# The norm before the MLP in a two-layer encoder kernel: transposes of the residual's second half grouped in four PSUM banks between halves of up tiles, and the first weight sums moved behind the third up tile

## The chip, the cores and the metric

One core of one Trainium2 chip. The metric is device time in microseconds (us) of one execution; the median of 3 runs of the kernel before is 1730.86 us (1730.69 to 1731.39). The engines are PE (TensorE: matrix products and transposes), DVE (VectorE), ACT (ScalarE), POOL (GpSimd), and SP, whose queue issues most weight loads.

## The reference, cut to what matters

Two layers, 512 positions of 1024 channels, float32. Of each layer only its end matters here:

```python
merged = (gates[:, :, 0] * (y_a @ w_br[l, 0]) + gates[:, :, 1] * (y_b @ w_br[l, 1])
          + gates[:, :, 2] * (y_c @ w_br[l, 2]))
x = x + merged @ w_out[l]
hn = rms_norm(x, ln2[l])
x = x + jnp.square(jax.nn.relu(hn @ w_up[l])) @ w_down[l]
```

`w_up` is 1024x4096 and `w_down` 4096x1024. `rms_norm` divides each row by its root mean square and multiplies by a weight per channel.

## The kernel before, in words

**Products.** Every float32 operand is split in a high and a low part (`split`, `wsplit`): ACT rounds the value to the matmul's format (the high part, `xh`, `wh`), DVE subtracts that from the value (the low part, `xl`, `wl`). A product is then three matmuls, high by high, low by high and high by low (`mm3`, lines 212 to 214). A weight chunk of 128x1024 is loaded by SP (`wr`, line 187; 2 buffers), cast by ACT (line 207) and subtracted by DVE (line 208) into a pair `wh`, `wl` (3 buffers each).

**The residual and its norm.** `proj_tok` makes `merged @ w_out` by halves of 512 channels (`fl` 0 and 1), in four PSUM banks, one for each 128 positions. DVE adds each bank to the residual `xr` (line 1108), ACT takes sums of squares (line 314). The MLP needs the residual with channels on the partitions, so `turn` (line 316) transposes it on PE: a half gives 4 tiles `xT` of 128x512, each from 4 transposes of 128x128 (line 327) into one PSUM bank. Of each tile ACT makes `xh` (line 265) and DVE `xl` (line 266), both reading the bank, which is free for another tile after that. The first half goes through the two banks with the tag `c`, the second through the two banks with the tag `s`. PSUM has 8 banks here: two each of tags `m`, `a`, `c`, `s`.

**The MLP.** The 4096 hidden channels go in four quarters (`qd`), each of 8 up tiles (`f` 0 to 7) and then a down product. An up tile is a PSUM bank of 128 hidden channels by 512 positions, the sum over `k` of 8 channel tiles, 24 matmuls of 128x512, in a bank of tag `m`: tiles `k` 0 to 3 come from the residual's first half and 4 to 7 from its second. ACT takes Relu and Square (lines 1171, 1172), and `left_first` / `left_second` make splits and sums of the squares for the down product, which is a seven-product scheme (Strassen's) over 2x2 blocks. That scheme also needs sums of the blocks of the down weights. Those are 8 chunks `wq`, loaded by `uload` on SP's queue (line 197); their pool opens when `Y2`, which holds the operand of `w_out`, is closed. `early_sums` (lines 403 and 405) makes 4 sums of 128x1024 of them on DVE, in place or into two further buffers.

**What sets the order.** Each engine runs its instructions in a fixed order, which a scheduler decides as the program is built, from its own estimate of a timeline and from priorities (`hp()` raises one). `tc.issue_after(x)`, which the change uses, is a context whose instructions are ordered behind instruction `x` on their engine. In the order before, up tiles 0 and 1 of the first quarter are interleaved with each other and with the transposes of the second half, and the 4 early sums stand on DVE among the 4 `xl` of that half. The source calls `early_sums` after up tile 4.

Of the kernel before, what the change touches and what calls it, by code (L numbers as in the profile page):

```python
# [6 lines left out]
F32 = mybir.dt.float32  # L7
# [3 lines left out]
ALU = mybir.AluOpType  # L11

P = 128
S = 512
D = 1024
KT = D // P
# [13 lines left out]
def ap_of(t, off, dims):  # L30
    return bass.AP(tensor=t.tensor, offset=t.offset + off, ap=[t.ap[0]] + dims)
# [29 lines left out]
def trunk(tc, xT, xt, ws, vec, fnb, bsb, snk, wst, rope, cmask, amask, ident, out):  # L61
    nc = tc.nc
# [52 lines left out]
    def Z():  # L115
        z4[1] += 1
        return z4[0][:, (z4[1] - 1) % 4]
# [4 lines left out]
    def SM(tag, w):  # L122
        return pad.tile([P, w], F32, tag="sm_" + tag, bufs=4 if tag == "lb" else NSM, name=nm(tag))
# [4 lines left out]
    def PT(tag, name):  # L128
        return ps.tile([P, S], F32, tag="p_" + tag, bufs=BANKS[tag], name=nm(name))
# [3 lines left out]
    def hp():  # L133

        return tc.high_priority() if boost[0] else contextlib.nullcontext()
# [36 lines left out]
    def ln_ap(which, l, kt):  # L172
        c = {"ln1": 0, "ln2": 16, "fn": 32}[which] + (l * 8 if which != "fn" else 0) + kt
        return vec_t[:, c:c + 1]
# [7 lines left out]
    def wload(*key):  # L182
        if key in ready:
            return ready.pop(key)
        with hp():
            raw = sb.tile([P, CW], F32, tag="wr", bufs=WR, name=nm("wr"))
            nc.sync.dma_start(raw, ws[CHUNK[key]])
            return wsplit(raw)
# [12 lines left out]
    def whl():  # L201
        return (sb.tile([P, CW], F32R, tag="wh", bufs=WB, name=nm("wh")),
                sb.tile([P, CW], F32R, tag="wl", bufs=WB, name=nm("wl")))

    def wsplit(raw):
        hi, lo = whl()
        nc.scalar.copy(hi, raw)  # L207
        nc.vector.tensor_tensor(lo, raw, hi.bitcast(F32), ALU.subtract)  # L208
        return hi, lo

    def mm3(pt, whi, wlo, xhi, xlo, first, last):
        nc.tensor.matmul(pt, whi, xhi, start=first, stop=False)  # L212
        nc.tensor.matmul(pt, whi, xlo, start=False, stop=False)  # L213
        nc.tensor.matmul(pt, wlo, xhi, start=False, stop=last)  # L214

    def proj(xs, name, *key, bank="m"):

        return proj_w(xs, name, wload(*key), bank=bank)

    def proj_w(xs, name, w, koff=0, bank="m"):  # L220
        hi, lo = w
        pt = PT(bank, name)
        for k, x in enumerate(xs):
            c = slice((koff + k) * P, (koff + k + 1) * P)
            mm3(pt, hi[:, c], lo[:, c], x[0], x[1], k == 0, k == len(xs) - 1)
        return pt
# [32 lines left out]
    def split(src, hi, lo, scale=None):  # L259

        if scale is None:
            nc.scalar.copy(hi, src)  # L262
            nc.vector.tensor_tensor(lo, src, hi.bitcast(F32), ALU.subtract)
        else:
            nc.scalar.activation(hi, src, AF.Copy, scale=scale)
            nc.vector.scalar_tensor_tensor(lo, src, scale, hi.bitcast(F32), ALU.mult, ALU.subtract)  # L266


    def rstd_c(pt, n):
# [36 lines left out]
    def norm_tok(which, l, xr, keep):  # L306

        n = Norm()
        n.xs, n.xf = [None] * KT, [None] * KT
        n.ss = SM("ss8", 8)  # L310

        def add(t, fl):
            j = T("jk", "jk")
            nc.scalar.activation(j, xr[t][fl], AF.Square, accum_out=n.ss[:, t * 2 + fl:t * 2 + fl + 1])

        def turn(fl, ts, bank="s"):

            w = len(ts) * P
            c0 = ts[0] * P
            for d in range(4 * fl, 4 * fl + 4):  # L320
                if n.xs[d] is None:
                    n.xs[d] = (T("x", "xh", F32R), T("x", "xl", F32R))
                    if keep:
                        n.xf[d] = Z() if d < 4 else T("l", "xf")
                pt = PT(bank, "xT")
                for i, t in enumerate(ts):
                    nc.tensor.transpose(pt[:, i * P:(i + 1) * P], xr[t][fl][:, (d % 4) * P:(d % 4 + 1) * P], id_t)
                src = pt[:, 0:w]
                parts = [x[:, c0:c0 + w] for x in n.xs[d]]
                if keep:  # L330
                    xf = n.xf[d][:, c0:c0 + w]
                    nc.scalar.activation(xf, src, AF.Copy, scale=ln_ap(which, l, d))
                    split(xf, *parts)
                else:
                    split(src, *parts, ln_ap(which, l, d))

        def end():
            s = SM("s4", 4)
            nc.vector.tensor_tensor(s, ap_of(n.ss, 0, [[2, 4]]), ap_of(n.ss, 1, [[2, 4]]), ALU.add)
            n.rc = rstd_c(s, D)  # L340

        n.add, n.turn, n.end = add, turn, end
        return n

# [8 lines left out]
    HT = 2 * P  # L353
# [4 lines left out]
    def left_first(new, u):  # L358

        p1 = new().rearrange("p (a b) -> p a b", a=2)  # L360
        split(u[:, 0:HT], p1[:, 0], p1[:, 1])
        sb_ = part["wq"].tile([P, 2, HT], F32, tag="sf", bufs=2, name=nm("sf"))
        nc.vector.tensor_tensor(sb_[:, 0], u[:, 0:HT], u[:, HT:], ALU.subtract)
        return {1: (p1[:, 0], p1[:, 1]), "u": u, "s": sb_}

    def left_second(new, h, v):
        V = nc.vector
# [32 lines left out]
    def early_sums(raw):  # L400
        b11, b12, b22, b21, t1 = raw
        for i in range(2):
            nc.vector.tensor_tensor(t1[i], b11[i], b12[i], ALU.add)
        for i in range(2):
            nc.vector.tensor_tensor(b12[i], b12[i], b22[i], ALU.add)
# [267 lines left out]
    raw, hi, lo = sb.tile([P, CW], F32, tag="wr", bufs=WR, name=nm("wr")), *whl()  # L673
    for i in range(2):
        c = slice(i * S, (i + 1) * S)
# [26 lines left out]
    for l in range(DEPTH):  # L702
        xs = n1.xs
# [53 lines left out]
        if l == 0:  # L757
            raw = uload(l, "un", 0)
# [62 lines left out]
        for u in range(3):  # L821
# [7 lines left out]
            raw = nxt  # L829
# [40 lines left out]
        for g in range(4):  # L870
            pt = PT("s", "mx")
# [64 lines left out]
        pt = PT("c", "vT")  # L936
# [162 lines left out]
        xr = [[T("l", "xr"), T("l", "xr")] for _ in range(4)]  # L1099
# [3 lines left out]
        n2 = norm_tok("ln2", l, xr, False)  # L1103
        for fl in range(2):
            pts = proj_tok(ms, "wo", (l, "wo", fl), fl, None if fl else lambda: turn_sum(1))
            for t in range(4):
                with hp():
                    nc.vector.scalar_tensor_tensor(xr[t][fl], pts[t], 0.5, xr[t][fl], ALU.mult, ALU.add)
                    n2.add(t, fl)
            with hp():  # L1110
                n2.turn(fl, range(4), "s" if fl else "c")
        with hp():
            n2.end()
        r2 = SM("r2", 4)
        nc.vector.tensor_tensor(r2, n2.rc, n2.rc, ALU.mult)
        nr2 = SM("r2", 4)
# [7 lines left out]
        last = l + 1 == DEPTH  # L1124
# [33 lines left out]
        for qd in range(4):  # L1158
            hs, nh = [], [0]

            def new():
                nh[0] += 1
                return T("jk" if nh[0] == 1 else "rb" if nh[0] > 27 else "l2" if nh[0] > 23 else "h", "sh", F32R)

            for f in range(8):
                pt = proj(n2.xs, f'up{qd}', l, "up", qd, f)
                if f == 0:
                    raw = uload(l, "dn", qd)
                u = Z()
                with hp():  # L1170
                    nc.scalar.activation(u, pt, AF.Relu)  # L1171
                    nc.scalar.activation(u, u, AF.Square)
                    if f % 2 == 0:
                        hs.append(left_first(new, u))
                    else:
                        left_second(new, hs[-1], u)
                if f == 4:
                    early_sums(raw)
            if qd == 3:
                if last:  # L1180
                    for fl in range(2):
                        fn_t.append(Z())
                        nc.sync.dma_start(fn_t[fl], bass.AP(tensor=fnb.tensor, offset=fnb.offset + fl * S, ap=[[0, P], [1, S]]))
                else:
                    nxt = uload(l + 1, "un", 0)
            down(qd, raw, hs, acc, xr, r2, nr2, done, last)
        if not last:
            with hp():
                n1.end()
            raw = nxt  # L1190
# [125 lines left out]
```

## Time and profile before

| | |
|---|---|
| median of 3 runs | 1730.86 us (1730.69 to 1731.39) |
| span of the profiled execution, first to last instruction | 1729.5 us |
| PE busy | 1685.3 us, 97% of the span |
| DVE busy | 1297.1 us, 75% |
| ACT busy | 1017.1 us, 59% |
| mean granted PE clock | 0.996 |
| up matmuls in both layers | 1536, about 390 ns each by the profile, 227 ns from start to start |

For the profiled execution the page gives the span; the median of the runs is 1.36 us above it, and that difference is taken as what lies around the span. Columns of the time tables that follow: a timeline row has start, duration, engine, line, operation, output<-inputs, the tile's form and the count of merged instructions, and in brackets how long the engine sat idle before and what ended that. A matmul's duration includes its way through the array, so starts are compared rather than durations added. A windows row has the length of the stretch, then busy time and count for PE, PEld (weight loads into the array), DVE, ACT and POOL, then the granted PE clock, the DMA share and GB/s.

### The profile page before, as it was taken

Reading aid. Unit: us, or ns where it says so; the run is one execution under the profiler, and the core shown is the slowest. Engines: PE = TensorE matmul, PEld = TensorE weight load, DVE = VectorE, ACT = ScalarE, POOL = GpSimd, SP = SyncE. Lnnn points to the kernel's source line nnn. Section 1 sums busy time; section 2 is a strip of 40 time slices with the busy share of each in tenths; the row PEclk is TensorE's granted clock in tenths of the full one; section 3 lists DMA queues with packets and bytes.
Section 4 is the critical chain, followed back from the end, with each engine's and each line's share of the span. In section 5 each row is a group of like instructions: output and inputs, shape, how many; then the busy total and the mean of one; then the engine's idle time right before and its main releaser. Section 6 shows DMA issues by size and latency. Waiting matters only on the chain.

```text
span 1729.5 us, 21976 instructions
## 1 busy us (share of the span) xinstructions
PE 1685.3 (97%) x8024; PEld 1405.0 (81%) x8024; DVE 1297.1 (75%) x2009; ACT 1017.1 (59%) x1715; POOL 146.1 (8%) x215
## 2 busy tenths in 40 slices
PE   8999999999999999999999999999999999999997
PEld 7888878887877888888888787888877878888886
DVE  7996977687566668686889869876776567686867
ACT  7665567677335555545665754877772355545454
POOL 0011200000310000000010112000004000000001
PEclk9999999999999999999999999999999999999999
DMA  8342232231545332233423422322317353232311
GB/s 331 98 146 92 83 104 81 72 104 55 203 187 182 98 110 98 98 98 98 134 92 126 147 93 71 104 79 75 111 48 273 130 182 98 98 98 97 119 65 49
DMA packets 58283, 200.04 MB, mean 116 GB/s; under 512 B 7904, under 2 KB 8288, under 8 KB 58176
## 3 DMA queue, kind: packets, MB, share of 16 engines
q1 hardware_dynamic: 44640, 154.72, 26.6%
q0 software_dynamic: 13248, 43.40, 6.7%
q8 instruction: 63, 1.03, 0.3%
q10 hardware_dynamic: 288, 0.52, 0.1%
q14 instruction: 44, 0.36, 0.1%
HBM read 177.64 MB, written 20.97 MB: 115 GB/s over the span
## 4 chain that ended last, share of the span: by engine, by line
PE 43%; issue 20%; DVE 4%; ACT 2%; POOL 0%; POOLq 0%; ACTq 0%; DVEq 0%
PE up L213 3%; PE up L212 3%; PE up L214 3%; PE dA L418 2%; PE dA L420 2%; PE dA L419 2%; PE at L558 1%; PE gA L418 1%; PE gz L214 1%; PE gz L213 1%; PE gz L212 1%; PE dC L418 1%; PE dC L420 1%; PE dC L419 1%; PE gA L420 1%
## 5 line engine op out<-in xcount | busy, mean ns | idle before, releaser
L207 ACT CAST wh<-wq 128x1024 fp32r<-128x1024 f32 x201 | 211.4, 1052 | 208.2 <-PE up L213 49.3
L208 DVE TENSOR_TENSOR wl<-wq,wh 128x1024 fp32r<-128x1024 f32 x201 | 245.1, 1222 | 117.1 <-ACT wh L207 116.1
L208 DVE TENSOR_TENSOR wl<-wr,wh 128x1024 fp32r<-128x1024 f32 x166 | 203.9, 1228 | 148.0 <-ACT wh L207 147.6
L207 ACT CAST wh<-wr 128x1024 fp32r<-128x1024 f32 x166 | 174.0, 1049 | 214.6 <-PE up L213 67.3
L212 PE MATMUL up<-xh,wh 128*128 128x512 f32 x512 | 199.2, 390 | 1.9 <-ACT u L1171 1.9
L213 PE MATMUL up<-xl,wh 128*128 128x512 f32 x512 | 200.6, 392 | 0.1
L214 PE MATMUL up<-xh,wl 128*128 128x512 f32 x512 | 199.1, 391 | 0.0
L212 PEld LDWEIGHTS up<-xh,wh 128*128 128x128 f32 x512 | 96.3, 188 | 22.7 <-ACT u L1171 2.7
L213 PEld LDWEIGHTS up<-xl,wh 128*128 128x128 f32 x512 | 96.4, 188 | 20.3 <-DVE xl L266 0.6
L214 PEld LDWEIGHTS up<-xh,wl 128*128 128x128 f32 x512 | 96.5, 189 | 19.8
L418 PE MATMUL dA<-wh,sh 128*128 128x512 f32 x256 | 99.8, 390 | 0.0
L419 PE MATMUL dA<-wh,sh 128*128 128x512 f32 x256 | 99.7, 389 | 0.0
L420 PE MATMUL dA<-wl,sh 128*128 128x512 f32 x256 | 92.6, 390 | 0.0
L600 DVE TENSOR_TENSOR ex<-ex 128x512 f32<-128x512 f32 x112 | 78.1, 715 | 6.3 <-ACT kt L575 5.4
L558 PEld LDWEIGHTS at<-qt,kt 128*128 128x128 f32 x448 | 57.0, 191 | 9.9 <-ACT kt L575 4.7
L558 PE MATMUL at<-qt,kt 128*128 128x128 f32 x448 | 59.6, 276 | 5.6 <-DVE qt L573 2.7
L572 ACT ACTIVATE qt<-ex 128x512 f32<-128x512 f32 x56 | 37.7, 674 | 46.3 <-DVE ex L600 38.5
L274 POOL TENSOR_TENSOR rs<-ms,mhalf_t 128x4 f32<-128x4 f32 (+2 forms) x15 | 17.3, 1156 | 530.6 <-DVE ms L272 527.5
L420 PEld LDWEIGHTS dA<-wl,sh 128*128 128x128 f32 x256 | 48.1, 188 | 10.0
L418 PEld LDWEIGHTS dA<-wh,sh 128*128 128x128 f32 x256 | 48.1, 188 | 10.0
L419 PEld LDWEIGHTS dA<-wh,sh 128*128 128x128 f32 x256 | 48.1, 188 | 9.9
L262 ACT CAST sh<-sf 128x512 fp32r<-128x512 f32 x64 | 39.7, 621 | 24.3 <-DVE sf L383 18.0
(403 smaller groups left out, 4403.0 us busy)
## 6 DMA issues: line engine op xcount, KB each, us to landing
wr<-in_ws_dram SPq DMA_DIRECT2D x166, 512.0 KB, 3.3
wq<-in_ws_dram SPq DMA_DIRECT2D x117, 512.0 KB, 4.3
thd<-zt POOLq DMA_DIRECT2D x32, 256.0 KB, 2.5
th<-thd POOLq DMA_DIRECT2D x32, 256.0 KB, 4.6
mgd<-mg POOLq DMA_DIRECT2D x16, 256.0 KB, 2.9
mcd<-th POOLq DMA_DIRECT2D x16, 256.0 KB, 2.5
mC<-mcd POOLq DMA_DIRECT2D x16, 256.0 KB, 6.7
mB<-mgd POOLq DMA_DIRECT2D x16, 256.0 KB, 6.6
```

The source lines that it names most:

```text
L207: nc.scalar.copy(hi, raw)
L208: nc.vector.tensor_tensor(lo, raw, hi.bitcast(F32), ALU.subtract)
L212: nc.tensor.matmul(pt, whi, xhi, start=first, stop=False)
L213: nc.tensor.matmul(pt, whi, xlo, start=False, stop=False)
L214: nc.tensor.matmul(pt, wlo, xhi, start=False, stop=last)
L262: nc.scalar.copy(hi, src)
L418: nc.tensor.matmul(pt, xh[:, t], hi[:, c], start=start and k == 0, stop=False, skip_group_check=True)
L419: nc.tensor.matmul(pt, xl[:, t], hi[:, c], start=False, stop=False, skip_group_check=True)
L420: nc.tensor.matmul(pt, xh[:, t], lo[:, c], start=False, stop=k == 3, skip_group_check=True)
L558: nc.tensor.matmul(pt[:, c], kk(st), qq[:, c], start=True, stop=True)
L572: nc.scalar.activation(qt.rearrange(shp, b=nb, h=2), e_q, AF.Exp)
L600: nc.vector.tensor_tensor(o_ap, o_ap, ap_of(ex, i_, [[istep, 2]] + z), ALU.add)
```

## The change

- `turn` takes a string of four bank tags instead of one tag. The first half still uses `c` four times. The second half uses `ssaa`: four banks, so that each of its 4 tiles has a bank of its own.
- The first three up tiles of the first quarter are cut in halves: `proj_part` issues the matmuls of some `k` alone. In program order come the first half (`k` 0 to 3) of up tile 0, then the 16 transposes of the residual's second half ordered behind it, then the first halves of tiles 1 and 2 ordered behind the transposes. The second halves (`k` 4 to 7) follow inside the usual loop over `f`. Each of the three tiles keeps its weight pair until its second half.
- Up tiles 2 and 3 of the first quarter lie in banks of tag `c`, the others in `m`.
- In the first quarter `early_sums` is called after up tile 6 and ordered behind the first subtraction of `left_first` for up tile 2 (`hs[1]["i"]`); in the others it stays after tile 4.
- This stands once in each layer.

```diff
+    def proj_part(xs, pt, w, ks):
+        hi, lo = w
+        for k in ks:
+            c = slice(k * P, (k + 1) * P)
+            i = mm3(pt, hi[:, c], lo[:, c], xs[k][0], xs[k][1], k == 0, k == KT - 1)
+        return i
...
-        def turn(fl, ts, bank="s"):
+        def turn(fl, ts, banks="ssss"):
...
-                pt = PT(bank, "xT")
+                pt = PT(banks[d % 4], "xT")
...
-            with hp():
-                n2.turn(fl, range(4), "s" if fl else "c")
+            if fl == 0:
+                with hp():
+                    n2.turn(0, range(4), "cccc")
+        first = [(PT("m", "up0"), wload(l, "up", 0, 0))]
+        i = proj_part(n2.xs, *first[0], range(4))
+        with hp(), tc.issue_after(i.ins):
+            tp = n2.turn(1, range(4), "ssaa")
         with hp():
             n2.end()
+        with tc.issue_after(tp.ins):
+            for f in (1, 2):
+                first.append((PT("c" if f == 2 else "m", "up0"), wload(l, "up", 0, f)))
+                proj_part(n2.xs, *first[f], range(4))
...
-                pt = proj(n2.xs, f'up{qd}', l, "up", qd, f)
+                if qd == 0 and f < 3:
+                    pt = first[f][0]
+                    proj_part(n2.xs, *first[f], range(4, KT))
+                else:
+                    pt = proj(n2.xs, f'up{qd}', l, "up", qd, f, bank="c" if qd == 0 and f == 3 else "m")
...
-                if f == 4:
-                    early_sums(raw)
+                if f == (6 if qd == 0 else 4):
+                    with tc.issue_after(hs[1]["i"].ins) if qd == 0 else contextlib.nullcontext():
+                        early_sums(raw)
```

How the instructions move. On PE, before, in the first layer, around the third group of transposes. `up_1098` and `up_1082` are up tiles 1 and 0, `xh_4663` is the last tile of the first half and `xh_4808` the first of the second half:

```order
L212 MATMUL up_1098_4934<-xh_4663,wh_4930 128x512
L213 MATMUL up_1098_4934<-xl_4664,wh_4930 128x512
L214 MATMUL up_1098_4934<-xh_4663,wl_4931 128x512
L212 MATMUL up_1082_4878<-xh_4808,wh_4874 128x512
L212 MATMUL up_1098_4934<-xh_4808,wh_4930 128x512
L327 MATMUL xT_4828<-id_t,xr_4436 128x128
L327 MATMUL xT_4828<-id_t,xr_4438 128x128
L327 MATMUL xT_4828<-id_t,xr_4440 128x128
L327 MATMUL xT_4828<-id_t,xr_4442 128x128
L213 MATMUL up_1082_4878<-xl_4809,wh_4874 128x512
```

The third tile's transposes stand behind matmuls that use the first transposed tile, and ahead of the ones that use its low part. On PE, after the change, at the end of the 16 transposes (`up_1069` is up tile 1, `xh_4636` and `xh_4645` are of the first half):

```order
L335 MATMUL xT_4838<-id_t,xr_4440 128x128
L335 MATMUL xT_4838<-id_t,xr_4442 128x128
L335 MATMUL xT_4847<-id_t,xr_4442 128x128
L335 MATMUL xT_4856<-id_t,xr_4442 128x128
L212 MATMUL up_1069_4869<-xh_4636,wh_4872 128x512
L213 MATMUL up_1069_4869<-xl_4637,wh_4872 128x512
L214 MATMUL up_1069_4869<-xh_4636,wl_4873 128x512
L212 MATMUL up_1069_4869<-xh_4645,wh_4872 128x512
```

All four tiles' transposes now stand together, and what follows them needs only the first half. Behind it 24 first-half matmuls of up tiles 1 and 2 stand ahead of the first that uses a tile of the second half.

On DVE, before, the same place (`s`, `ms`, `r` are the norm's small operations, L403 and L405 the early sums, `wl_5018` the low weights of up tile 3):

```order
L339 TENSOR_TENSOR s_1062_4844<-ss_981_4451 128x4
L272 TENSOR_SCALAR ms_4846<-s_1062_4844 128x4
L1115 TENSOR_TENSOR r_1065_4850<-rs_4848 128x4
L1117 TENSOR_SCALAR r_1066_4852<-r_1065_4850 128x4
L403 TENSOR_TENSOR wq_4919<-wq_4903,wq_4907 128x1024
L266 SCALAR_TENSOR_TENSOR xl_4809<-xT_4810,vec_t,xh_4808 128x512
L266 SCALAR_TENSOR_TENSOR xl_4818<-xT_4819,vec_t,xh_4817 128x512
L403 TENSOR_TENSOR wq_4920<-wq_4905,wq_4909 128x1024
L405 TENSOR_TENSOR wq_4907<-wq_4907,wq_4911 128x1024
L266 SCALAR_TENSOR_TENSOR xl_4827<-xT_4828,vec_t,xh_4826 128x512
L405 TENSOR_TENSOR wq_4909<-wq_4909,wq_4913 128x1024
L266 SCALAR_TENSOR_TENSOR xl_4836<-xT_4837,vec_t,xh_4835 128x512
```

On DVE, after the change, from the norm's last operation on:

```order
L1136 TENSOR_SCALAR r_1078_4909<-r_1077_4907 128x4
L274 SCALAR_TENSOR_TENSOR xl_4828<-xT_4829,vec_t,xh_4827 128x512
L274 SCALAR_TENSOR_TENSOR xl_4837<-xT_4838,vec_t,xh_4836 128x512
L274 SCALAR_TENSOR_TENSOR xl_4846<-xT_4847,vec_t,xh_4845 128x512
L274 SCALAR_TENSOR_TENSOR xl_4855<-xT_4856,vec_t,xh_4854 128x512
L208 TENSOR_TENSOR wl_5018<-wr_5015,wh_5017 128x1024
L372 TENSOR_TENSOR sf_4964<-u_4919 128x256
```

The four `xl` stand together behind the norm. The early sums (L412 and L414 now) start 12 rows after `wl_5018`, behind the first subtraction of up tile 2 (`sf_5013`), with the low weights of up tile 6 (`wl_5154`) among them:

```order
L208 TENSOR_TENSOR wl_5105<-wr_5102,wh_5104 128x1024
L271 TENSOR_TENSOR sh_4988<-sf_4984,sh_4987 128x512
L271 TENSOR_TENSOR sh_4993<-sf_4964,sh_4992 128x512
L372 TENSOR_TENSOR sf_5013<-u_4919 128x256
L412 TENSOR_TENSOR wq_4957<-wq_4941,wq_4945 128x1024
L412 TENSOR_TENSOR wq_4958<-wq_4943,wq_4947 128x1024
L271 TENSOR_TENSOR sh_5010<-u_4919,sh_5010 128x256
L414 TENSOR_TENSOR wq_4945<-wq_4945,wq_4949 128x1024
L208 TENSOR_TENSOR wl_5154<-wr_5151,wh_5153 128x1024
L414 TENSOR_TENSOR wq_4947<-wq_4947,wq_4951 128x1024
```

The orders of POOL and of SP's queue are as before. The second layer has the same moves; outside these two places no engine's order differs.

More of the change, by code (lines that the diff above doesn't have):

```diff
@@ L213, in mm3 @@
         nc.tensor.matmul(pt, whi, xlo, start=False, stop=False)
-        nc.tensor.matmul(pt, wlo, xhi, start=False, stop=last)
+        return nc.tensor.matmul(pt, wlo, xhi, start=False, stop=last)
+    def proj_part(xs, pt, w, ks):
[4 more added lines that the diff above has]
+        return i
     def proj(xs, name, *key, bank="m"):
@@ L262, in split @@
             nc.scalar.copy(hi, src)
-            nc.vector.tensor_tensor(lo, src, hi.bitcast(F32), ALU.subtract)
+            return nc.vector.tensor_tensor(lo, src, hi.bitcast(F32), ALU.subtract)
         else:
             nc.scalar.activation(hi, src, AF.Copy, scale=scale)
-            nc.vector.scalar_tensor_tensor(lo, src, scale, hi.bitcast(F32), ALU.mult, ALU.subtract)
+            return nc.vector.scalar_tensor_tensor(lo, src, scale, hi.bitcast(F32), ALU.mult, ALU.subtract)
     def rstd_c(pt, n):
@@ L324, in turn @@
                         n.xf[d] = Z() if d < 4 else T("l", "xf")
-                pt = PT(bank, "xT")
+                pt = PT(banks[d % 4], "xT")
                 for i, t in enumerate(ts):
-                    nc.tensor.transpose(pt[:, i * P:(i + 1) * P], xr[t][fl][:, (d % 4) * P:(d % 4 + 1) * P], id_t)
+                    tp = nc.tensor.transpose(pt[:, i * P:(i + 1) * P], xr[t][fl][:, (d % 4) * P:(d % 4 + 1) * P], id_t)
                 src = pt[:, 0:w]
@@ L335, in turn @@
                     split(src, *parts, ln_ap(which, l, d))
+            return tp
         def end():
@@ L362, in left_first @@
         sb_ = part["wq"].tile([P, 2, HT], F32, tag="sf", bufs=2, name=nm("sf"))
-        nc.vector.tensor_tensor(sb_[:, 0], u[:, 0:HT], u[:, HT:], ALU.subtract)
-        return {1: (p1[:, 0], p1[:, 1]), "u": u, "s": sb_}
+        i = nc.vector.tensor_tensor(sb_[:, 0], u[:, 0:HT], u[:, HT:], ALU.subtract)
+        return {"i": i, 1: (p1[:, 0], p1[:, 1]), "u": u, "s": sb_}
     def left_second(new, h, v):
```

## Prediction

> **What bounds the kernel now.** I read PE's busy share first, then PE's own waits, then a table by stretches around the change, then the time tables of PE, DVE and ACT there. The page's head, and from the waits of PE the two that the change touches (total us, times, longest):
>
> ```profile
> span 1729.5 us, 21976 instructions
> PE 1685.3 (97%) x8024; PEld 1405.0 (81%) x8024; DVE 1297.1 (75%) x2009; ACT 1017.1 (59%) x1715; POOL 146.1 (8%) x215
> ...
> PE xT L327 <- DVE xl L266: 4.7, 2, 2.4
> PE up L212 <- ACT u L1171: 1.9, 2, 1.0
> ```
>
> PE is the bound, so time that PE loses here is lost to the kernel. Twice, once a layer, PE stands at a transpose until DVE has made an `xl`; and once a layer the third up tile waits for ACT's Relu, which frees a bank `m`. Stretches, the first three in the first layer, the last two in the second:
>
> ```profile
> 528.60:533.10 4.50, 4.50 (x21) 3.69 (x20) 2.62 (x7) 2.69 (x7) 1.04 (x1) 1.00 0.71 259
> 533.10:537.80 4.70, 2.43 (x15) 1.82 (x13) 2.08 (x4) 1.27 (x2) 0.00 (x0) 1.00 0.97 377
> 537.80:545.30 7.50, 6.44 (x30) 4.70 (x30) 5.83 (x7) 2.96 (x5) 0.00 (x0) 1.00 0.58 238
> ...
> 1391.10:1396.00 4.90, 2.53 (x17) 1.86 (x14) 2.16 (x5) 1.27 (x2) 0.00 (x0) 1.00 0.97 381
> ...
> 1397.10:1400.80 3.70, 3.70 (x13) 2.93 (x12) 3.70 (x5) 0.93 (x2) 0.00 (x0) 0.54 0.85 347
> ```
>
> PE is busy for 2.43 of 4.70 us while the transfers run at 377 GB/s, and in the second layer a stretch at a granted clock of 0.54 follows. The reason stands in DVE's time table of the first layer:
>
> ```profile
> 526.74 2.73 DVE L1108 SCALAR_TENSOR_TENSOR xr<-wo,xr 128x512 f32<-128x512 f32 x4 [1.31 <-PE wo L256]
> 529.98 1.23 DVE L208 TENSOR_TENSOR wl<-wr,wh 128x1024 fp32r<-128x1024 f32 x1 [0.51 <-ACT wh L207]
> ...
> 533.08 0.17 DVE L1117 TENSOR_SCALAR r<-r 128x4 f32<-128x4 f32 x1
> 535.87 1.22 DVE L403 TENSOR_TENSOR wq<-wq,wq 128x1024 f32<-128x1024 f32 x1 [2.62 <-DMA wq<-in_ws_dram]
> 537.01 1.40 DVE L266 SCALAR_TENSOR_TENSOR xl<-xT,vec_t,xh 128x512 fp32r<-128x512 f32 x2
> ...
> 542.39 0.74 DVE L266 SCALAR_TENSOR_TENSOR xl<-xT,vec_t,xh 128x512 fp32r<-128x512 f32 x1
> 544.80 1.23 DVE L208 TENSOR_TENSOR wl<-wr,wh 128x1024 fp32r<-128x1024 f32 x1 [1.67 <-ACT wh L207]
> ```
>
> An early sum (L403) waits 2.62 us for down weights that are still on their way, and the two `xl` behind it wait with it; the other three sums hold the last two `xl` back to 543.13. Only when an `xl` is done is a bank `s` free for the third transposed tile. The chain is: weight transfer, early sum, `xl`, bank, transposes, last `xl`, up tiles 0 and 1, cast and Relu, up tile 2.
>
> **What PE needs in this place.** From the time tables of PE, first layer:
>
> ```profile
> 528.58 0.39 PE L212 MATMUL up<-xh,wh 128*128 128x512 f32 x1
> ...
> 533.12 1.03 PE L327 MATMUL xT<-id_t,xr 128*128 128x128 f32 x8
> 533.91 0.48 PE L214 MATMUL up<-xh,wl 128*128 128x512 f32 x1
> 534.22 0.40 PE L212 MATMUL up<-xh,wh 128*128 128x512 f32 x1
> ...
> 537.81 0.66 PE L327 MATMUL xT<-id_t,xr 128*128 128x128 f32 x4 [2.28 <-DVE xl L266]
> ...
> 545.32 0.50 PE L212 MATMUL up<-xh,wh 128*128 128x512 f32 x1 [0.93 <-ACT u L1171]
> ...
> 550.89 0.39 PE L212 MATMUL up<-xh,wh 128*128 128x512 f32 x1
> ```
>
> and second layer:
>
> ```profile
> 1386.64 0.39 PE L212 MATMUL up<-xh,wh 128*128 128x512 f32 x1
> ...
> 1395.96 0.66 PE L327 MATMUL xT<-id_t,xr 128*128 128x128 f32 x4 [2.37 <-DVE xl L266]
> ...
> 1410.20 0.39 PE L212 MATMUL up<-xh,wh 128*128 128x512 f32 x1
> ```
>
> The first row of each is the first up matmul, the last the first matmul of up tile 3 (24 behind 545.32). Between them lie three up tiles, 72 matmuls, and 16 transposes, before and after the change alike. They take 550.89 - 528.58 = 22.31 us and 1410.20 - 1386.64 = 23.56 us. Without a wait: 20 matmuls lie between 528.58 and 533.12, so 4.54 / 20 = 0.227 us each; 8 transposes take 533.91 - 533.12 = 0.79 us, 0.099 each; the first matmul behind them takes 0.31 us to the next start, 0.08 more. So 72 x 0.227 + 16 x 0.099 + 0.08 = 16.34 + 1.58 + 0.08 = 18.00 us.
>
> **The change part by part.** *Four banks and the grouping.* The `xT` no longer wait for each other's banks. Their two `a` and two `s` banks come free with the four additions to `xr`, which end at 526.74 + 2.73 = 529.47. PE reaches the transposes 12 matmuls after 528.58, at 531.30, 1.8 us later, and is through at 532.9. The price of 16 in a row is not in the trace; 0.099 each is that of 8 in a row. From above, the load of their weights takes 0.139 us each (below), or 0.64 us more a layer; from below nothing is gained, since 8 in a row run without a gap.
>
> *The first halves as cover.* Tiles 1 and 2 give 24 matmuls, 5.45 us, so tile 0's second half is due at 532.98 + 5.45 = 538.4. What must be done by then is on ACT and DVE:
>
> ```profile
> L327 PEld LDWEIGHTS xT<-id_t,xr x16: 138/139/142, 532.9 to 539.9; 128*128 128x128 f32 x16
> ...
> 528.91 1.04 ACT L207 CAST wh<-wr 128x1024 fp32r<-128x1024 f32 x1
> ...
> 533.75 1.27 ACT L265 ACTIVATE xh<-xT,vec_t 128x512 fp32r<-128x512 f32 x2 [2.43 <-PE xT L327]
> ...
> 543.73 1.05 ACT L207 CAST wh<-wr 128x1024 fp32r<-128x1024 f32 x1 [2.71 <-PE up L213]
> ...
> 549.85 0.62 ACT L262 CAST sh<-sf 128x512 fp32r<-128x512 f32 x1 [0.32 <-DVE sf L386]
> 550.87 1.05 ACT L207 CAST wh<-wr 128x1024 fp32r<-128x1024 f32 x1 [0.40 <-PE up L213]
> 551.82 0.59 ACT L1171 ACTIVATE u<-up 128x512 f32<-128x512 f32 x1
> 552.44 0.63 ACT L1172 ACTIVATE u<-u 128x512 f32<-128x512 f32 x1
> ```
>
> Now ACT starts 0.63 us after the first of the group of transposes (533.75 - 533.12), with four of the eight behind it. After the change the first tile's last transpose is the tenth (its four, and six of others), so ACT starts at 531.30 + 0.63 + 6 x 0.099 = 532.5; four `xh` at 1.27 / 2 end at 535.1. DVE is free from 533.25 (its `r` ends then) and makes four `xl` at 0.70 behind them, the last by 536.2. That is 2.2 us ahead of need. Weights of tiles 1 and 2 are there: the cast of the third pair ran at 528.91 and its low part ended at 531.21, both before the down weights matter. If this cover failed by its whole length, PE would wait 2.4 us as now.
>
> *Three weight pairs held.* Tile 3's cast needs tile 0's pair, read until tile 0 ends at 538.4 + 2.72 = 541.1 (the cast at 550.87 starts as the third tile's matmuls end, 550.89). Cast 1.05 and low part 1.23 with some 0.15 between give 543.5; tile 3 is due at 528.58 + 18.00 = 546.6. Margin 3.1 us. Later tiles have one whole tile more. Tile 3's bank `c` has been free since the first half's transposes, so the 0.93 us wait for a Relu goes; tile 4's bank `m` is free with tile 0's Relu near 542.7 and is due at 552.0.
>
> *The early sums, later.* They are 4 x 1.22 = 4.9 us of DVE. DVE now, between the low weights of tile 3 and the cast's release for the first down weights, and SP's loads:
>
> ```profile
> 544.80:567.20 22.40, 21.88 (x96) 18.13 (x97) 14.35 (x23) 14.23 (x24) 0.00 (x0) 1.00 0.36 118
> ...
> 528.77 3.55 SPq L197 DMA_DIRECT2D wq<-in_ws_dram  x7
> ...
> 546.06 18.36 SPq L187 DMA_DIRECT2D wr<-in_ws_dram  x5
> ...
> wr<-in_ws_dram SPq DMA_DIRECT2D x5, 512.0 KB, 3.4
> ```
>
> DVE is busy 14.35 of 22.40 us. After the change this stretch runs from 542.3 to the first down weights' low part near 564.1, 21.8 us, with 14.35 + 4.9 = 19.2 us to do: 2.6 us are left. Hidden, then, though narrowly. The sums can start near 551.3, an estimate: tile 2 ends at 546.6, then ACT has a cast, Relu, Square and two splits, 1.05 + 0.59 + 0.63 + 2 x 0.62 = 3.5 us, and DVE is one split and one small subtraction behind, about 1.2. The DVE instruction that PE needs among the sums is tile 6's low weights: behind three sums, a split of about 0.4 and its own 1.23 it is done near 556.6, and tile 6 is due at 562.9. SP's queue keeps its order: its next `wr` is released by tile 3's low weights, at 543.5 and not 546.03, and lands 3.4 us later, 546.9, for tile 5, due at 557.4. The sums' operands land long before.
>
> **The sum.** First layer 22.31 - 18.00 = 4.31, second 23.56 - 18.00 = 5.56, together 9.87 us. Beyond up tile 3 the order is as before and PE was already without a wait there, so I let the gain reach the end. Span 1729.5 - 9.87 = 1719.6; the median of the runs lies 1.36 above the span, so **1721.0 us**.
>
> **A place where a rule could change this.** The second layer's 1.25 us more than the first come with the clock of 0.54, right behind an idle of 2.37 us; the first layer's idle of 2.28 us left the clock at 1.00. I count the slow stretch as a result of the wait, so it goes with it. The Trainium skill, page "TensorE: Matmul & The Clock Gate", section "What's actually happening", says that the clock is halved after at least one idle window of about 3.4 us, that windows run freely, and so that the moment differs between runs; no idle here is that long, and by that rule the wait would not be the cause. By it the sum would lose the second layer's extra.
>
> **The rivals.** *The clock drop stays.* If it comes in the second layer whatever PE waits for, that layer gains what the first does: 2 x 4.31 = 8.6, 1722.2 us. For it: two waits of nearly one length, only one with a drop. Against: it came within 1.2 us of the wait, and nowhere else in these stretches.
>
> *DVE is late with its work.* The 2.6 us left in that stretch may go to waits for ACT. Then part of the 4.9 us comes back as a wait, at most 4.9 - 2.6 = 2.3 a layer: 9.87 - 4.6 = 5.3 gained, 1725.6 us. Against: the weights that PE needs stand ahead of the sums or have 6 us.
>
> *The second half is no sooner.* If something else held the four `xl` until 543.1 as now, 36 matmuls of the second halves would follow, 543.1 + 8.17 = 551.3, 0.4 behind 550.89: 1731.6 us at most, no change that could be told. Against: nothing but the norm's small operations stands ahead of them.
>
> *Slower: the weights lose their lead.* All three pairs are held until the second halves are read. If tile 3's low weights came more than 3.1 us later than I find, PE would wait for them, and if the lead did not return, at each of tiles 3 to 7: cast and low part, 2.3 us, five times, 11.5 a layer, 23 in all, less 9.87: 13 us slower, 1744 us. Against: the cast is first in ACT's order there, behind the four `xh`.
>
> **How the numbers follow.** The forecast has 0.77, the clock drop 0.11, late DVE 0.05, no sooner 0.04, slower 0.03. No change is within 0.2% (3.5 us), about what this kernel's measurement can tell. So faster 0.77 + 0.11 + 0.05 = 0.93, same 0.04, slower 0.03. The range: below, 1.5 us for waits elsewhere and the runs' own spread of 0.7; above, the clock case at 1722.2 with the dear transposes (2 x 0.64) and 1 us for a short wait: 1719.5 to 1724.5.
>
> **What would show it.** Right: in PE's waits, no `xT` behind `xl` and no `up` behind `u` in either layer; 18.0 us from the first up matmul to that of tile 3, in both layers; the `xl` on DVE directly behind the norm; the early sums near 551 without a wait for a transfer; a clock of 1.00 throughout. Wrong: an `up` on L213 that waits for `xl`, on L212 for `wh`, a clock near 0.5 in the second layer, or a new wait in the first down product.

## The result, and the profile after

The changed kernel takes 1721.69 us (median of 5 runs, 1720.54 to 1723.07) against 1730.86 us before. The ratio is 0.9952, with a 95% interval of 0.994 to 0.9964: by the ratio 8.3 us less, 6.2 to 10.4; the two medians lie 9.17 us apart. The forecast was 1721.0. The profiled execution took 1720.54 us with a span of 1718.7 us.

PE's time table of the changed kernel at the same place, first layer and then second; first row the first up matmul, last row the first matmul of up tile 3:

```profile
527.63 0.39 PE L212 MATMUL up<-xh,wh 128*128 128x512 f32 x1
...
530.36 1.91 PE L335 MATMUL xT<-id_t,xr 128*128 128x128 f32 x16
532.02 0.48 PE L212 MATMUL up<-xh,wh 128*128 128x512 f32 x1
...
545.72 0.39 PE L212 MATMUL up<-xh,wh 128*128 128x512 f32 x1
...
1381.40 0.39 PE L212 MATMUL up<-xh,wh 128*128 128x512 f32 x1
...
1399.48 0.39 PE L212 MATMUL up<-xh,wh 128*128 128x512 f32 x1
```

The stage takes 18.09 us in the first layer and 18.08 in the second, where it took 22.31 and 23.56. The 16 transposes take 532.02 - 530.36 = 1.66 us. The table by stretches shows PE busy throughout both stages at full clock (18.10 of 18.10 us, 1.00):

```profile
527.60:545.70 18.10, 18.10 (x89) 15.21 (x88) 9.15 (x17) 10.43 (x19) 1.04 (x1) 1.00 0.77 291
1381.40:1399.50 18.10, 18.10 (x90) 15.23 (x89) 9.15 (x17) 10.43 (x19) 1.03 (x1) 1.00 0.76 291
```

DVE in the first layer, with the four `xl` in a row behind the norm's `r`, a free stretch, then tile 3's low weights and the early sums (L412, L414) with tile 6's low weights among them:

```profile
532.13 0.17 DVE L1136 TENSOR_SCALAR r<-r 128x4 f32<-128x4 f32 x1
532.37 2.72 DVE L274 SCALAR_TENSOR_TENSOR xl<-xT,vec_t,xh 128x512 fp32r<-128x512 f32 x4
541.34 1.23 DVE L208 TENSOR_TENSOR wl<-wr,wh 128x1024 fp32r<-128x1024 f32 x1 [6.25 <-ACT wh L207]
...
550.00 2.35 DVE L412 TENSOR_TENSOR wq<-wq,wq 128x1024 f32<-128x1024 f32 x2
...
553.74 1.22 DVE L208 TENSOR_TENSOR wl<-wr,wh 128x1024 fp32r<-128x1024 f32 x1
554.88 1.22 DVE L414 TENSOR_TENSOR wq<-wq,wq 128x1024 f32<-128x1024 f32 x1
```

The sums wait for no transfer now. **The balance of the two profiled spans** is 1729.5 - 1718.7 = 10.8 us: 4.22 from the first layer's stage, 5.48 from the second's, and 528.58 - 527.63 = 0.95 from work ahead of the first stage, where the change does nothing (see the last section). Outside the stages nothing else moved: from one stage's end to the next one's start it is 1386.64 - 550.89 = 835.75 us before and 1381.40 - 545.72 = 835.68 after, and behind the second stage 319.3 and 319.2 us remain.

### The profile page after: what moved, and what is told of

It is laid out like the page before. It is cut to its first block, busy times and chain, and to the rows that moved or that the text cites. A ratio compares the mean times of both kernels' runs of the same rounds, so it can differ in the third digit from the quotient of the medians.

```text
span 1718.7 us, 21970 instructions
## 1 busy us (share of the span) xinstructions
PE 1679.9 (98%) x8024; PEld 1402.0 (82%) x8024; DVE 1296.1 (75%) x2009; ACT 1016.7 (59%) x1715; POOL 146.3 (9%) x215
## 4 chain that ended last, share of the span: by engine, by line
PE 61%; issue 25%; DVE 8%; ACT 4%; POOL 1%; DMA 1%; POOLq 0%; SPq 0%; DVEq 0%; ACTq 0%
PE up L212 3%; PE up L214 3%; PE up L213 3%; PE at L567 2%; PE dA L427 2%; PE dA L429 2%; PE wo L264 2%; PE dA L428 2%; PE wo L263 2%; PE po L1006 2%; PE gz L214 2%; PE gz L212 2%; PE gz L213 2%; PE wo L262 2%; DVE ex L609 1%
## 5 line engine op out<-in xcount | busy, mean ns | idle before, releaser
L212 PE MATMUL up<-xh,wh 128*128 128x512 f32 x512 | 199.3, 389 | 0.0
L214 PE MATMUL up<-xh,wl 128*128 128x512 f32 x512 | 198.2, 389 | 0.0
L214 PEld LDWEIGHTS up<-xh,wl 128*128 128x128 f32 x512 | 96.1, 188 | 20.0
L212 PEld LDWEIGHTS up<-xh,wh 128*128 128x128 f32 x512 | 96.1, 188 | 19.9
L581 ACT ACTIVATE qt<-ex 128x512 f32<-128x512 f32 x56 | 37.8, 674 | 45.9 <-DVE ex L609 38.3
```

The source lines that it names most:

```text
L214: return nc.tensor.matmul(pt, wlo, xhi, start=False, stop=last)
L581: nc.scalar.activation(qt.rearrange(shp, b=nb, h=2), e_q, AF.Exp)
```

## The experiments

All stage lengths below run from the first up matmul to the first matmul of up tile 3, as in the forecast, and each run stands beside runs of the kernel before on the same chip. A loss can also fall behind that last row. Where it does, I give the length from the first up matmul to the first matmul of the down product (`dA`): it is 39.85 and 39.84 us in the changed kernel, and 44.07 and 45.32 in the forecast's profile of the kernel before.

**Early sums alone.** The kernel before with the early sums moved as in the change; two banks, whole up tiles.

```diff
-                if f == 4:
-                    early_sums(raw)
+                if f == (6 if qd == 0 else 4):
+                    with tc.issue_after(hs[1]["i"].ins) if qd == 0 else contextlib.nullcontext():
+                        early_sums(raw)
```

(`left_first` also returns that subtraction, as in the change.)

> Only the early sums are moved behind the third up tile; two banks, whole up tiles. Theory (the gain is the xl freed from the early sums' wait for a transfer, and what is left of the stall is bank and Relu waits): xl run directly behind the norm, no wait of PE at a transpose above 0.6 us, but the third up tile still waits about 1 us for ACT's Relu; from the first up matmul to that of tile 3 about 19.6 us in each layer against 22.3 and 23.6 before and 18.0 after; 5 to 7 us faster than before. Rival (the grouping in four banks or the halves make the gain): at most 1.5 us faster, 22 us stay.

PE's waits in its first layer's stage, between the stage's first and last row:

```profile
529.50 0.39 PE L212 MATMUL up<-xh,wh 128*128 128x512 f32 x1
...
543.34 0.50 PE L212 MATMUL up<-xh,wh 128*128 128x512 f32 x1 [0.95 <-ACT u L1171]
548.91 0.39 PE L212 MATMUL up<-xh,wh 128*128 128x512 f32 x1
```

19.41 us, 19.40 in the second layer. The wait at a transpose is gone, the one for the Relu stays. 1724.07 us against 1729.99, ratio 0.997 (0.996 to 0.998). As the theory has it: with two banks the sums' place was the cause of the wait at the transposes, but not of the whole stall.

**Four banks alone.** The kernel before with the transposes of the second half in `ssaa`; sums and tiles as they were.

```diff
-                n2.turn(fl, range(4), "s" if fl else "c")
+                n2.turn(fl, range(4), "ssaa" if fl else "cccc")
```

(`turn` takes the string of tags, as in the change.)

> Only the four banks: the second half's transposes use s, s, a, a; sums where they were, whole up tiles. In the order the transposes stand together and the early sums still among the xl. Theory: the first sum still waits for the transfer until about 535.9 in the first layer's time, but the transposes no longer wait for it; PE waits 0.5 to 1 us at a low-part matmul and about 1 us for the Relu: about 20.2 us in the stage, 4 to 5.5 us faster than before in both layers. Rival (the sums' wait is the whole stall): 22 us stay, at most 1 us faster.

```profile
529.42 0.39 PE L212 MATMUL up<-xh,wh 128*128 128x512 f32 x1
...
543.58 0.50 PE L212 MATMUL up<-xh,wh 128*128 128x512 f32 x1 [0.95 <-ACT u L1171]
549.15 0.39 PE L212 MATMUL up<-xh,wh 128*128 128x512 f32 x1
```

19.73 us, and 19.92 in the second layer with a wait of 0.25 us at an `xl`. 1724.98 us against 1729.99, ratio 0.9972 (0.9961 to 0.9982). So banks alone take the wait at the transposes away almost as well as the sums alone. The wait at a low part, expected at 0.5 to 1 us, was 0.25 us at most.

**Both, without halves.** Sums moved and four banks, all up tiles whole and in banks `m`.

> Early sums moved and four banks, but all up tiles in banks m and no halves. Theory: no wait at an xl, and what is left is the third up tile's wait for the Relu: 0.93 us with about 0.4 us of restart around it: stage 19.3 to 19.6 us. Rival (the Relu wait belongs to the late xl and goes with them): 18.3 us or less.

```profile
529.84 0.39 PE L212 MATMUL up<-xh,wh 128*128 128x512 f32 x1
...
543.64 0.50 PE L212 MATMUL up<-xh,wh 128*128 128x512 f32 x1 [0.95 <-ACT u L1171]
549.22 0.39 PE L212 MATMUL up<-xh,wh 128*128 128x512 f32 x1
```

19.38 us in both layers; one run, 1726.34 us. Together they give no more than the sums alone did. What is left is 19.38 - 18.09 = 1.3 us: the Relu wait and the restart around it, which go in the next run.

**A third bank added, still no halves.** The run above, with up tiles 2 and 3 in banks `c`.

```diff
-                pt = proj(n2.xs, f'up{qd}', l, "up", qd, f)
+                pt = proj(n2.xs, f'up{qd}', l, "up", qd, f, bank="c" if qd == 0 and f in (2, 3) else "m")
```

> Early sums moved, four banks, and up tiles 2 and 3 in banks c, but no halves: whole up tiles, which the scheduler interleaves. Theory: with a third bank the scheduler itself puts the third tile's first-half matmuls ahead of the second halves, the xl are done in time and no Relu is waited for: stage 18.0 to 18.3 us, time within 1 us of the changed kernel. Rival (the halves written out are what covers the xl): PE waits of 1 us or more at L213 or L212 in the stage, 19 us or more, 2 us slower than the changed kernel.

```profile
528.31 0.39 PE L212 MATMUL up<-xh,wh 128*128 128x512 f32 x1
...
546.44 0.39 PE L212 MATMUL up<-xh,wh 128*128 128x512 f32 x1
```

18.13 and 18.12 us, no wait in either stage, 1722.05 us against 1729.99, ratio 0.9958 (0.9943 to 0.9973). The theory holds: once a third bank is there, the scheduler interleaves the third tile by itself, and the halves written out in the source add nothing that can be measured. ("A third bank" is short for this edit: tiles 2 and 3 take one of the two banks `c` each. What tile 3's own bank is worth was not tried apart.)

**The third bank alone.** The kernel before with only that one line of edit.

> The kernel before with one edit: up tiles 2 and 3 of the first quarter lie in banks c instead of m. The scheduler then puts tile 2's first-half matmuls ahead of the second halves; the sums stay among the xl and the transposes in two banks. Theory (what PE lacked was other work to do until the xl come, and a third bank gives it): PE reaches the third transposes about 9.7 us behind the first up matmul, the first xl is done near 9.2, and only the last xl, behind all four sums, may be late by up to 1 us: stage 18.2 to 19.2 us, 5 to 8 us faster than before. Rival (the xl have to be freed, by moved sums or by four banks): a wait at a transpose of 1 us or more stays, stage 20 us or more, at most 4 us faster.

DVE and then PE in the first layer's stage, where DVE's first row is an early sum that waits for the transfer as before:

```profile
533.91 1.22 DVE L403 TENSOR_TENSOR wq<-wq,wq 128x1024 f32<-128x1024 f32 x1 [1.78 <-DMA wq<-in_ws_dram]
535.06 1.40 DVE L266 SCALAR_TENSOR_TENSOR xl<-xT,vec_t,xh 128x512 fp32r<-128x512 f32 x2
...
537.51 2.35 DVE L405 TENSOR_TENSOR wq<-wq,wq 128x1024 f32<-128x1024 f32 x2
539.78 0.74 DVE L266 SCALAR_TENSOR_TENSOR xl<-xT,vec_t,xh 128x512 fp32r<-128x512 f32 x1
541.10 0.75 DVE L266 SCALAR_TENSOR_TENSOR xl<-xT,vec_t,xh 128x512 fp32r<-128x512 f32 x1 [0.58 <-ACT xh L265]
```

```profile
527.47 0.39 PE L212 MATMUL up<-xh,wh 128*128 128x512 f32 x1
...
537.23 0.60 PE L327 MATMUL xT<-id_t,xr 128*128 128x128 f32 x4
...
545.83 0.50 PE L212 MATMUL up<-xh,wh 128*128 128x512 f32 x1
547.09 0.50 PE L214 MATMUL up<-xh,wl 128*128 128x512 f32 x1 [0.53 <-DVE wl L208]
...
568.57 0.39 PE L418 MATMUL dA<-wh,sh 128*128 128x512 f32 x1
```

The same last row in the changed kernel, whose first up matmul starts at 527.63:

```profile
567.48 0.39 PE L427 MATMUL dA<-wh,sh 128*128 128x512 f32 x1
```

18.36 and 18.35 us, with no wait of PE inside the stage, although the sum still waits 1.78 us and the last two `xl` still stand behind all four sums. 1722.52 us against 1731.02, ratio 0.9949 (0.9931 to 0.9967). The last two `xl` end 13.05 and 14.38 us behind the first up matmul, the last one hardly sooner than the 14.55 before; PE has tile 2's first half to do meanwhile. In this profile the down weights also came rather early, with the first sum at 6.4 us behind the first up matmul where the profiles of the kernel before have 6.2 to 7.8; PE reached the third tile's transposes about 1.5 us behind the first `xl`, which would cover that span.

The wait at L214 is new: up tiles 0 to 2 end nearly together, so their weight pairs come free late, and tile 3 waits 0.53 us for its low weights. It lies behind the row that ends the stage, so the 18.36 us leave it out. To the first matmul of the down product this run takes 568.57 - 527.47 = 41.10 us, 1.25 more than the changed kernel, and 41.09 in the second layer. That is as long as with the sums alone (41.17 and 41.16). By the profiles, then, the third bank alone is worth as much as the sums alone and less than the change; the runs' times are too few and scattered to tell it from the change.

**Third bank with one other part.** One run each: with four banks, and with the sums moved.

> Four banks for the transposes and banks c for up tiles 2 and 3; the sums stay where they were, no halves. Theory: stage 18.0 to 18.4 us with no wait at an xl, although the first sum still waits for its transfer on DVE. Rival (the sums' wait must go): a wait of 1 us or more at a low-part matmul, 19 us or more.

> Early sums moved and banks c for up tiles 2 and 3; transposes in two banks, no halves. Theory: the third and fourth transposes stand behind tile 2's first half, and their banks are free by then: stage 18.0 to 18.5 us. Rival (two banks hold PE up, as in the run with the changed kernel on two banks): 19 us or more.

18.13 us in both layers with four banks (1720.07 us), 18.34 and 18.33 us with the sums moved (1723.07 us), the latter again with 0.53 us at tile 3's low weights. Neither has a wait at an `xl`. To the first matmul of the down product the first takes 39.89 us in both layers, the second 41.06 and 41.03. What four banks add to the third bank is that tile 3's wait goes. So these two, without moved sums or halves, already bring what the whole change brings, by one profile.

**The changed kernel with the sums left in place.** The last hunk of the diff undone.

> The changed kernel with the early sums left where they were called, after up tile 4; in DVE's order the first sum then stands behind two of the four xl and ahead of the other two. Theory: that sum waits for the transfer to about 7.3 us behind the first up matmul and the last xl is done near 9.9 us, but the halves of tiles 1 and 2 put the need for it at 11.2 to 11.9 us, so no wait: stage 18.0 to 18.3 us, within 0.5 us of the changed kernel. Rival (the sums' place is what counts, as in the forecast's chain of waits): a wait of PE at an xl of 1 us or more, stage 19.5 us or more, 3 us slower than the changed kernel.

DVE in the first layer's stage, whose first up matmul starts at 528.00:

```profile
532.74 1.41 DVE L274 SCALAR_TENSOR_TENSOR xl<-xT,vec_t,xh 128x512 fp32r<-128x512 f32 x2
535.29 1.23 DVE L412 TENSOR_TENSOR wq<-wq,wq 128x1024 f32<-128x1024 f32 x1 [1.14 <-DMA wq<-in_ws_dram]
536.43 1.41 DVE L274 SCALAR_TENSOR_TENSOR xl<-xT,vec_t,xh 128x512 fp32r<-128x512 f32 x2
```

18.09 us in both layers, 1721.81 us against 1729.6, ratio 0.9952 (0.9934 to 0.997). An early sum holds two `xl` back as in the forecast's chain, and PE never notices. The last `xl` ends at 536.43 + 1.41 = 537.84, 9.84 us behind the first up matmul, as expected.

**The changed kernel with two banks.** `ssss` in place of `ssaa`.

> The changed kernel with the second half's transposes in two banks (s four times). Theory: the third tile's transposes wait for the first xl, made near 2.1 us behind the first transpose, so PE loses 1.2 to 1.5 us in each layer: stage 19.2 to 19.5 us, 2.4 to 3 us slower than the changed kernel, 6.5 to 7.5 faster than before. Rival (with the sums gone from between, two banks are enough): stage 18.2 or less, within 0.5 us of the changed kernel.

```profile
528.62 0.39 PE L212 MATMUL up<-xh,wh 128*128 128x512 f32 x1
...
532.72 0.49 PE L212 MATMUL up<-xh,wh 128*128 128x512 f32 x1 [0.34 <-ACT xh L273]
533.51 0.66 PE L335 MATMUL xT<-id_t,xr 128*128 128x128 f32 x4 [0.29 <-DVE xl L274]
...
547.85 0.39 PE L212 MATMUL up<-xh,wh 128*128 128x512 f32 x1
```

19.23 and 19.22 us; 1724.18 us against 1729.99, ratio 0.9971 (0.9958 to 0.9983), 2.5 us above the changed kernel's median. With the transposes ordered ahead of the other halves, the four banks are needed; with tile 2's first half ahead of them (the third bank alone) they were not. The medians lie 5.8 us apart, short of the 6.5 to 7.5 expected. That expectation took the stages of the kernel before from its first profile; against the average of three (below, under the sum), 44.32 - 38.45 = 5.87 us are what the stages give.

**The changed kernel without cover.** Tile 0's second half directly behind the transposes.

```diff
         with tc.issue_after(tp.ins):
-            for f in (1, 2):
-                first.append((PT("c" if f == 2 else "m", "up0"), wload(l, "up", 0, f)))
+            i = proj_part(n2.xs, *first[0], range(4, KT))
+        for f in (1, 2):
+            first.append((PT("c" if f == 2 else "m", "up0"), wload(l, "up", 0, f)))
+        with tc.issue_after(i.ins):
+            for f in (1, 2):
                 proj_part(n2.xs, *first[f], range(4))
...
                     pt = first[f][0]
-                    proj_part(n2.xs, *first[f], range(4, KT))
+                    if f:
+                        proj_part(n2.xs, *first[f], range(4, KT))
```

> The changed kernel with up tile 0's second half ordered directly behind the 16 transposes, ahead of the first halves of tiles 1 and 2: the same work, without the 24 matmuls between. Theory: ACT's first xh is done 0.3 to 0.5 us behind the last transpose and DVE's first xl 1.1 us behind it; after that ACT and DVE keep pace with PE, so PE loses 1.0 to 1.3 us a layer: stage 19.0 to 19.4 us, 2 to 2.6 us slower than the changed kernel. Rival (the cover is not needed at all once the xl are free): stage 18.4 us or less. Other rival (the whole row of four xl must be waited for): 3 us a layer, stage 21 us.

```profile
533.31 0.50 PE L212 MATMUL up<-xh,wh 128*128 128x512 f32 x1
534.10 0.50 PE L213 MATMUL up<-xl,wh 128*128 128x512 f32 x1 [0.28 <-DVE xl L274]
```

19.06 and 19.09 us, with a wait of 0.28 us at an `xl`; 1723.48 us against 1729.6, ratio 0.9961 (0.9949 to 0.9973). The 24 matmuls of cover are worth 0.97 and 1.01 us, at the low end of the 1.0 to 1.3 expected: the rest of the row of `xl` keeps pace with PE. The loss is larger than the idle time in brackets, since the starts around it are further apart: 534.10 - 533.31 = 0.79 us where 0.227 would do.

**The kernel before, profiled twice more.**

> The kernel before, profiled again, for the second layer's clock drop. Theory (the drop depends on how the wait lies against windows of fixed length, so it differs from run to run): the waits stay at 2.3 and 2.4 us, but the granted clock need not fall in the second layer's stage; where it does not fall the stage takes 22.3 us as in the first layer. Rival (the wait of the second layer brings the drop each time): clock near 0.5 behind the wait and 23.5 us again.

> The same once more, with the same expectations: two further profiles of the kernel before, to be set beside the first one's 22.31 and 23.56 us.

The waits at the transposes and the first sum's wait, of the first of the two profiles (first layer, second layer):

```profile
539.37 0.66 PE L327 MATMUL xT<-id_t,xr 128*128 128x128 f32 x4 [2.77 <-DVE xl L266]
...
1395.89 0.65 PE L327 MATMUL xT<-id_t,xr 128*128 128x128 f32 x4 [1.14 <-DVE xl L266]
```

```profile
537.43 1.22 DVE L403 TENSOR_TENSOR wq<-wq,wq 128x1024 f32<-128x1024 f32 x1 [3.11 <-DMA wq<-in_ws_dram]
...
1393.95 1.23 DVE L403 TENSOR_TENSOR wq<-wq,wq 128x1024 f32<-128x1024 f32 x1 [1.50 <-DMA wq<-in_ws_dram]
```

and the second layer's stretch behind the wait there, at full clock:

```profile
1395.00:1403.00 8.00, 6.43 (x30) 4.70 (x30) 6.33 (x9) 2.57 (x4) 0.00 (x0) 1.00 0.74 303
```

Stages of 22.83 and 21.23 us, and 21.52 and 21.51 us in the other profile (waits of 1.48 and 1.47). The clock did not fall in any of these four stages, not behind the 2.77 us either, though the drop of the first profile came behind 2.37. So a wait of this length does not bring the drop each time. The rival as it was worded, for the second layer, is not settled by that: the waits there were 1.14 and 1.47 us this time.

The expectation that the waits stay at 2.3 to 2.4 us failed: they ran from 1.14 to 2.77, with the landing of the down weights. In all six stages of the three profiles PE's wait at the transposes is 0.34 to 0.36 us shorter than the first sum's wait for the transfer (3.11 and 2.77, 1.50 and 1.14 above; 2.62 and 2.28 in the forecast's profile), as the forecast's chain from transfer to PE has it.

## Why the prediction was right, point by point

- *What PE needs in this place*, 18.00 us: measured 18.09 and 18.08. The transposes took 1.66 us where 1.58 + 0.08 had been worked out.
- *Four banks and the grouping; the first halves as cover.* Expected: the last `xl` at 536.2, 7.6 us behind the first up matmul. In the profile after, DVE's row of `xl` ends at 532.37 + 2.72 = 535.09, 7.46 us behind 527.63. No wait.
- *Three weight pairs held.* Expected a margin of 3.1 us at tile 3; its low weights ended at 541.34 + 1.23 = 542.57, 3.15 us ahead of 545.72. The mechanism of the slower rival exists all the same: with tile 0 kept open longer, in the third-bank run, tile 3 waits 0.53 us for its low weights in each layer.
- *The early sums, later.* Expected start near 551.3 in the time of the profile before, 22.7 us behind the first up matmul; it came at 550.00, 22.4 behind. Tile 6's low weights were done at 554.96, with no wait of PE. DVE was expected to have 19.2 us of work in the 21.8 us up to the first down weights; it had 18.60 in 21.76, and PE waited for none of it, so the rival of a late DVE did not come:

```profile
541.34:563.10 21.76, 21.76 (x98) 18.02 (x97) 18.60 (x28) 15.11 (x25) 0.00 (x0) 1.00 0.37 125
```

- *The sum.* The forecast subtracted 9.87 us and the ratio says 8.3 (6.2 to 10.4). 9.87 lies inside that interval, but the profiles say it is too much. The mis-sized term is the stall of the kernel before, taken from one execution as 22.31 + 23.56 us. Three profiles give 45.87, 44.06 and 43.03, on average 44.32, which is 8.15 us more than the 36.17 after. The first profile had the longest stall of the three, by its transfers and by a clock drop in the second stage. The forecast of the time suffers little from that, since it subtracts from the span of the same execution, where the long stall is counted too: 1729.5 less the measured 45.87 - 36.17 = 9.70 is 1719.8. The 1.36 us added to the span were too little: they set the median of three runs against the span of a single execution. In each of the other 13 profiled runs the time lies 1.8 us above the span, which gives 1721.6. That this is within 0.1 us of the median measured is luck too, for the changed kernel's five runs spread over 2.5 us.
- *The rule on the clock.* The row showed a drop behind an idle of 2.37 us; I took the drop as the wait's result and counted its 1.25 us in full. It came in one of six such stages, though only one of the other five waits, 2.77 us, was as long as the 2.37. The Trainium skill, page "TensorE: Matmul & The Clock Gate", section "What's actually happening", says that the windows run freely and the moment differs between runs; the repeated profiles agree so far as the drop came in some executions and not in others, and read that way only a share of the 1.25 us should have been counted. The Trainium skill's figure there, an idle window of about 3.4 us, is not borne out: the drop came with idles of 2.37 and 2.91 us here.
- *Which part did it.* The prediction told one chain, from the sum's wait to PE, and let the three parts each break a link. The experiments show that they overlap. To the first matmul of the down product the sums alone and both together take 41.1 to 41.2 us, four banks alone 41.5 and 41.7, the third bank alone 41.1, and the whole change 39.85. Four banks with the third bank reach 39.89, and with four banks and the halves the sums may stay where they were. So the parts shorten or cover the same wait, their gains do not add up, and the sums' move, which the prediction put beside the others, is not needed once the other parts are there.

What stays open: why the down weights land earlier in some executions than in others, and how often a wait of 2.4 us brings the clock down.

## What to carry to other kernels

When the bound engine waits behind a chain on another engine, look first for work that it could do meanwhile and for what keeps that work out; here banks of their own for the next tiles, in one line, were worth as much as freeing the chain of the early sums, and with four banks for the transposes as much as the whole change. A stage's length can leave out a wait that moved behind its last row, so a second, later end belongs beside it. A stall that ends with a DMA's landing, or that may bring a clock drop, should be sized from several executions: here three profiles gave 43.0 to 45.9 us for the same two stages.

## What the runs showed of the hardware

The same wait does not always bring the clock down. Ahead of the stage, at L212 `q`, PE waits for DVE. In the kernel before and in the changed kernel:

```profile
219.67 0.80 PE L212 MATMUL q<-xh,wh 128*128 128x512 f32 x1 [2.91 <-DVE z L717]
```

```profile
218.74 0.50 PE L212 MATMUL q<-xh,wh 128*128 128x512 f32 x1 [2.91 <-DVE z L726]
```

The idle is 2.91 us in both, and the matmul behind it takes 0.80 us in one and 0.50 in the other. The table by stretches of the kernel before has a clock of 0.51 for 3.4 us there, that of the changed kernel 1.00:

```profile
219.50:222.90 3.40, 3.23 (x8) 2.56 (x9) 3.34 (x6) 0.00 (x0) 0.00 (x0) 0.51 0.34 118
```

```profile
219.00:222.00 3.00, 3.00 (x14) 2.44 (x14) 2.94 (x5) 0.00 (x0) 0.00 (x0) 1.00 0.36 109
```

That lies ahead of the stage in both. It does not explain the 0.95 us by which the changed kernel's first up matmul comes sooner: 219.67 - 218.74 = 0.93 us of it are there before the drop, and 0.84 already at the first matmul of `f`, in the kernel before and then in the changed one:

```profile
30.31 0.39 PE L212 MATMUL f<-xh,wh 128*128 128x512 f32 x1
```

```profile
29.47 0.39 PE L212 MATMUL f<-xh,wh 128*128 128x512 f32 x1
```

From that `q` to the first up matmul it is 308.91 us with the drop and 308.89 without. The 14 profiles on record, of all the kernels here, agree. PE's idle ahead of `q` is 2.84 to 2.92 us in each; 12 have a drop there, which by the clock's own record in the trace lasts 3.41 us in seven and 6.83 us in five. From `q` to the first up matmul, the two without a drop and the seven with the short one take 308.86 to 308.99 us, the five with the long one 309.93 to 310.19. So the short drop cost nothing here and the long one about 1.1 us. DVE is busy for 3.34 of the 3.40 us above, which fits that PE had time to spare; no run was made to show it.
